# A fused SSD and attention layer: transposing normalised tokens, and V and dt as float32r products

## The chip, the cores and the metric

The kernel runs on one core of one Trainium2 chip. The metric is the device time of one execution in microseconds (us); shown are the median of three runs and their ends. The engines are called as in the profile: PE (matrix products, with PEld for its weight loads), DVE (vector), ACT (scalar), POOL (GpSimd) and SP (which only issues transfers here).

## The reference, cut

One layer over 512 tokens of width 1024, batch 1. A norm and one wide projection feed a two-way state-space scan (SSD) and a windowed attention; their outputs are gated, merged, projected and added to x; a squared-ReLU MLP follows. The change works on the first norm and on two of the projection's column groups, `dt_raw` and `v`.

```python
def rmsnorm(x, g):
    y = xf * lax.rsqrt(jnp.mean(xf * xf, axis=-1, keepdims=True) + EPS)
    return y * g

h = rmsnorm(x, pre_mix_norm[l])
proj = h @ w_in[l]
z, xbc, dt_raw, q, k, v, gates = split_cols(proj, IN_SPLITS)
y_ssd = ssd_branch(z, xbc, dt_raw, ..., w_ssd_out[l])
y_attn = window_attention(q, k, v, ...) @ w_attn_out[l]
mixed = (sigmoid(gates_ssd) * y_ssd + sigmoid(gates_attn) * y_attn) @ w_o[l]
x = x + rmsnorm(mixed, post_mix_norm[l])
f = square(relu(rmsnorm(x, pre_mlp_norm[l]) @ w_mlp_in[l])) @ w_mlp_out[l]
x = x + rmsnorm(f, post_mlp_norm[l])
```

## The kernel before

**Products.** Activations stand transposed, 128 features by 512 tokens per tile, eight tiles for a width of 1024. Nearly every large product is made from float32r operands: each operand is split into a high part (a cast to float32r on ACT, line 404 or 465) and a low part (the original less the high part, on DVE at line 405 or on POOL at line 469), and `mm3` (line 393) adds three products, high by high, high by low, low by high. V and dt are plain float32 products.

**Order.** The program is a list of quanta (groups of matmuls with the weights they need). `prefetch` loads weight chunks of 512 KB on SP's queue into a ring of three raw tiles and splits them into rings `wh` and `wl` of three. A Planner (line 64) then takes all instructions, costs them, lists them for each engine, and `chain` (line 490) fixes that order by dependencies. Working tiles of 128 x 512 come from 83 numbered slots.

**The start.** `start` (line 538) sends the identity and the norm's weight over ACT's queue, x and the four pieces `wv` of the V weights over SP's, and lets PE multiply zeros 20 times. For each of four token tiles, `turn_x` (line 583) transposes raw x in eight pieces, and ACT and DVE scale each by the norm's weight, which stands per partition in `gT`, into `xg` (lines 594, 596). `norm_x` (line 598) makes sums of squares on ACT and DVE and the reciprocal root `rst` on POOL (lines 608, 609). `v_quantum` (line 706) multiplies `xg` by `wv`, 32 products of 128 x 256, and scales by `rst` on the way out (line 722). `normal_h` (line 611) spreads `rst` over a tile `ra`, transposes it, multiplies it with `xg` and splits into `h`, in pieces of 128 x 256. `dt_quantum` (line 728) makes 32 products of 64 columns from `xg`, and `dt_math` (line 748) scales them by `rst`. Behind dt come the projection's other columns in chunks, K first.

**The seam to y.** When the last projection columns are done, the 16 slots of `h` are given back, and `split_y` (line 1246) splits the scan's output `yT` (16 tiles) into `yh` and `yl` (lines 1254, 1255) for the product with `w_ssd_out`. `flip_h2` (line 1366) fills 16 slots `h2`, the MLP's input, later.

## Time and profile before

| | us |
|---|---|
| median of three runs | 1096.55 |
| lowest, highest | 1095.93, 1097.31 |
| the profiled execution | 1097.11 |
| its span in the profile | 1095.3 |
| PE, POOL, DVE, ACT busy in it | 1083.8, 771.3, 759.7, 640.5 |
| first product of a projection chunk | 34.37 |
| start of the products with y | 623.36 |

Times in the rows are microseconds from the start of the span unless marked ns. A row of the timeline reads: start, time taken, engine, line, operation, output and inputs by the program's names, shapes, count, and in brackets the idle time of the engine ahead of it and what ended it. A row of the view by groups has count, then busy time and the mean of one in ns, then idle time ahead. A row of the waits has the engine that waits, for whom, total us, times, longest.

### The profile page before, as it was taken

To read this page: it belongs to the slowest core of one execution; us is meant where nothing else is said; L and a number is where in the kernel's file an instruction comes from. 1 tells how busy PE (TensorE), PEld (TensorE's weight loads), DVE (VectorE), ACT (ScalarE), POOL (GpSimd) and SP (SyncE) were. 2 spreads that over 40 slices of the span, in tenths; PEclk is the share of its full clock that TensorE was granted. 3 is DMA by queue.
4 is the path that set the end of the run, shared out by engine and by line. 5 is a ranking of instruction groups with operands and counts; after the bars stand their busy time and mean duration, and the time that the engine had idled before them with its cause. 6 is when DMAs were issued, how large, how long until landed. Compare 5 with 4: busy or idle time off the path is not lost. (4 is left out here: it accounts for less than half of the span.)

```text
span 1095.3 us, 16847 instructions
## 1 busy us (share of the span) xinstructions
PE 1083.8 (99%) x5647; PEld 910.1 (83%) x5647; DVE 759.7 (69%) x1319; ACT 640.5 (58%) x1387; POOL 771.3 (70%) x960
## 2 busy tenths in 40 slices
PE   9999999999999999999999999999999999999997
PEld 8887888888888888888888878888888888888886
DVE  5777887888796787886878843335653655755787
ACT  6467777687766777676678622323655444444543
POOL 2446657657568898999899866523668978978853
PEclk9999999999999999999999999999999999999999
DMA  6443624535535546556574563534311621621532
GB/s 206 123 121 104 146 79 140 132 82 146 137 99 168 156 141 167 152 146 165 141 189 124 175 201 97 163 100 161 117 43 53 193 69 48 193 74 43 165 102 77
DMA packets 214658, 140.66 MB, mean 128 GB/s; under 512 B 11779, under 2 KB 193523, under 8 KB 214572
## 3 DMA queue, kind: packets, MB, share of 16 engines
q1 hardware_dynamic: 214412, 139.53, 44.8%
q8 instruction: 44, 0.72, 0.3%
q14 instruction: 42, 0.34, 0.1%
q10 hardware_dynamic: 160, 0.07, 0.0%
HBM read 130.85 MB, written 8.72 MB: 127 GB/s over the span
## 5 line engine op out<-in xcount | busy, mean ns | idle before, releaser
L469 POOL TENSOR_TENSOR wl<-wr,wh 128x256 fp32r<-128x256 f32 (+1 forms) x500 | 412.1, 853 | 161.0 <-ACT wh L465 151.7
L387 PE MATMUL pp<-h,wh 128*128 128x512 f32 (+1 forms) x1712 | 524.2, 387 | 0.5 <-DVE h L1350 0.5
L387 PEld LDWEIGHTS pp<-h,wh 128*128 128x128 f32 x1712 | 316.4, 188 | 63.3 <-issue 1.0
L387 PE MATMUL pp<-h,wl 128*128 128x512 f32 (+1 forms) x856 | 331.9, 388 | 0.0
L465 ACT CAST wh<-wr 128x1024 fp32r<-128x1024 f32 x131 | 136.4, 1041 | 91.2 <-PE pp L387 79.0
L387 PEld LDWEIGHTS pp<-h,wl 128*128 128x128 f32 x856 | 160.8, 188 | 32.2 <-issue 0.3
L1517 POOL TENSOR_TENSOR wl<-wd,wh 128x256 fp32r<-128x256 f32 x140 | 114.2, 845 | 34.8 <-ACT wh L1513 31.6
L1513 ACT CAST wh<-wd 128x512 fp32r<-128x512 f32 x80 | 47.2, 620 | 51.3 <-PE pp L387 18.2
L387 PE MATMUL ps<-wh,fh 128*128 128x512 f32 (+1 forms) x196 | 75.5, 385 | 0.5 <-DVE acc L1563 0.5
L387 PE MATMUL ps<-wl,fh 128*128 128x512 f32 (+1 forms) x196 | 75.4, 385 | 0.0
L387 PE MATMUL ps<-wh,fl 128*128 128x512 f32 (+1 forms) x196 | 75.4, 385 | 0.0
L1393 DVE SCALAR_TENSOR_TENSOR pp<-pp,r 128x512 f32<-128x512 f32 (+1 forms) x31 | 17.6, 567 | 65.2 <-ACT r L1390 65.2
L1132 ACT ACTIVATE n<-cb,tables 128x128 f32<-128x128 f32 x128 | 49.1, 390 | 16.7 <-DVE cb L1123 14.6
L1517 POOL TENSOR_TENSOR wl<-wt,wh 128x256 fp32r<-128x256 f32 x56 | 45.5, 848 | 8.6 <-ACT wh L1513 4.9
L387 PE MATMUL pp<-yl,wh 128*128 128x512 f32 x128 | 50.0, 390 | 1.0 <-DVE yl L1255 1.0
L1168 POOL TENSOR_TENSOR w<-w,E 128x256 f32<-128x256 f32 x48 | 42.1, 891 | 12.3 <-DVE w L1164 5.9
L964 DVE SCALAR_TENSOR_TENSOR u<-pp,cv,u 128x510 f32<-128x510 f32 (+1 forms) x64 | 47.7, 745 | 3.3 <-ACT u L960 2.1
L387 PE MATMUL pp<-yh,wh 128*128 128x512 f32 x128 | 49.8, 389 | 0.0
L387 PE MATMUL pp<-yh,wl 128*128 128x512 f32 x128 | 49.8, 389 | 0.0
L1133 ACT ACTIVATE m<-cb,tables 128x128 f32<-128x128 f32 x128 | 48.8, 388 | 0.0
L1062 POOL TENSOR_TENSOR xd<-x,tables 128x256 f32<-128x256 f32 x48 | 35.5, 757 | 17.6 <-ACT x L987 14.7
L884 ACT ACTIVATE P<-P,mx 128x384 f32<-128x384 f32 (+1 forms) x64 | 35.2, 552 | 17.5 <-DVE mx L881 12.4
(240 smaller groups left out, 2147.9 us busy)
## 6 DMA issues: line engine op xcount, KB each, us to landing
wr<-in_w_in SPq DMA_DIRECT2D x74, 512.0 KB, 4.3
wr<-in_w_mlp_in SPq DMA_DIRECT2D x32, 512.0 KB, 4.6
wd<-in_w_mlp_out SPq DMA_DIRECT2D x64, 256.0 KB, 2.6
rb<-csT SPq DMA_DIRECT2D x32, 256.0 KB, 4.6
rf<-csT SPq DMA_DIRECT2D x32, 256.0 KB, 5.5
wr<-in_w_ssd_out SPq DMA_DIRECT2D x14, 512.0 KB, 4.5
E<-csE SPq DMA_DIRECT2D x96, 64.0 KB, 4.1
x<-in_x SPq DMA_DIRECT2D x16, 256.0 KB, 4.8
```

The lines of the kernel that those rows point to most:

```text
L387: self.nc.tensor.matmul(out, lhsT, rhs, start=start, stop=stop, skip_group_check=more)
L465: self.nc.scalar.copy(hi[:, :m], raw)
L469: engines[e].tensor_tensor(lo[:, c], raw[:, c], hi[:, c].bitcast(F32), op=ALU.subtract)
L884: nc.scalar.activation(p[:, :w], p[:, :w], AF.Exp, bias=mx[:, n:n + 1], accum_out=sm[:, n:n + 1])
L964: nc.vector.scalar_tensor_tensor(u[:, a:e], ps[:, a + d:e + d], self.wtap(t, b), u[:, a:e], op0=ALU.mult, op1=ALU.add)
L1062: nc.gpsimd.tensor_tensor(v4(xd[:, d * 256:(d + 1) * 256]), v4(xs(c)), by_dir(self.coef, c)[:, d].unsqueeze(2).to_broadcast([128, 4, 64]), ...
L1132: nc.scalar.activation(v4(n)[:, h], cb[:, 0], AF.Copy, scale=dt[:, 0, h:h + 1])
L1133: nc.scalar.activation(v4(m)[:, h], cb[:, 1], AF.Copy, scale=dt[:, 1, h:h + 1])
L1168: nc.gpsimd.tensor_tensor(wc, wc, E[:, d], op=ALU.add)
L1393: nc.vector.scalar_tensor_tensor(dst[:, tok], ps[:, tok], 0.0, r[:, tok], op0=ALU.max, op1=ALU.mult)
L1513: nc.scalar.copy(hi, w)
L1517: (nc.vector if e == "v" else nc.gpsimd).tensor_tensor(low[:, q], w[:, q], hi[:, q].bitcast(F32), op=ALU.subtract)
```

## The change

The norm's weight is loaded as two rows of 512 and spread over all partitions by two products with a column of ones, into two banks `gb`. DVE multiplies x by its root and by `gb` in one instruction for 512 columns (into `junk`), and these normalised tokens are transposed. The results go straight from the banks, by a cast on ACT and a subtraction on DVE, into four wide tiles `b`, 128 x 4 x 512 each, two for the high parts of h and two for the low parts. `turn_x`, `normal_h`, `xg` and `gT` go away.

V is made from h by three float32r products, with `wv` split by a cast on ACT and a subtraction on POOL; dt by two, over a chunk that holds the high and low weights side by side (mode "both") and comes through the ring. The four wide tiles are taken again for tiles 6 to 13 of y and again for `h2`. There are 13 products of zeros in place of 20 and 67 slots in place of 83.

```diff
@@ -24,10 +24,10 @@
-SLOTS, RAW, SPL, PP, AHEAD, SPARE = 83, 3, 3, 3, 4, 6
+SLOTS, RAW, SPL, PP, AHEAD, SPARE = 67, 3, 3, 3, 4, 6
 LO_DOWN = "p", "p", "p", "vp"
-WARM = 20
+WARM = 10
...
@@ -424,6 +424,15 @@
     def add(self, *quanta):
         self.quanta.extend(quanta)
+    def wide(self):
+        t = []
+        for i in range(4):
+            a = self.sp.tile([128, 4, 512], F32R, tag=f"b{i}", name=self.name("b"), bufs=1)
+            self.tags[a.tensor.name] = f"b{i}", 1
+            t.append(a)
+        return t, [(t[k // 4][:, k % 4], t[2 + k // 4][:, k % 4]) for k in range(8)]
     def twin(self, name):
         return self.slots.get(name + "h", dtype=F32R), self.slots.get(name + "l", dtype=F32R)
@@ -540,15 +549,16 @@
         get, put = self.slots.get, self.slots.put
         self.ident = self.const("ident", [128, 128])
         nc.scalar.dma_start(self.ident, self.d_cst[:, :128])
-        g = get("g", (128, 128))
-        nc.scalar.dma_start(g[:8], self.d_pre_mix_norm[0].rearrange("(k p) -> k p", p=128))
+        g = [get("g") for _ in range(2)]
+        for j in range(2):
+            nc.scalar.dma_start(g[j][:1], self.d_pre_mix_norm[0:1, j * 512:(j + 1) * 512])
         self.mhalf = self.const("mhalf", [128, 1])
         nc.vector.memset(self.mhalf, -0.5)
         self.ssq0 = self.const("ssq0", [128, 8])
         self.rst0 = self.const("rst0", [128, 4])
-        self.gT = self.const("gT", [128, 8])
-        self.zero = get("zero", (128, 128))
+        self.zero, one = get("zero", (128, 128)), get("one", (128, 128))
         nc.vector.memset(self.zero, 0.0)
+        nc.vector.memset(one[:1], 1.0)
         dummy = self.bank("ps")
         for _ in range(WARM):
             self.mm(dummy[:, :128], self.zero, self.zero, True, True)
@@ -560,40 +570,28 @@
                 nc.sync.dma_start(self.x0[t][j], self.d_x[0, t * 128:(t + 1) * 128, j * 512:(j + 1) * 512])
         def load_v(k):
-            w = get("wv", (128, 2, 256))
+            w, hi, lo = (get("wv", (128, 2, 256), d) for d in (F32, F32R, F32R))
             nc.sync.dma_start(w, self.d_w_in[k * 128:(k + 2) * 128, C_V:C_V + 256].rearrange("(k p) n -> p k n", p=128))
-            self.wv.append(w)
+            nc.scalar.copy(hi, w)
+            nc.gpsimd.tensor_tensor(lo, w, hi.bitcast(F32), op=ALU.subtract)
+            put(w)
+            self.wv.append((hi, lo))
         load_x(0)
         for k in range(0, 8, 2):
             load_v(k)
         for t in range(1, NT):
             load_x(t)
-        pg = self.bank("ps")
-        self.tr(pg[:, :8], g[:8, :])
-        nc.vector.tensor_copy(self.gT, pg[:, :8])
-        put(g)
-        self.xg = [get("xg") for _ in range(8)]
-        self.h = [(get("h", dtype=F32R), get("h", dtype=F32R)) for _ in range(8)]
-        self.turn_x(0)
+        self.gb = [self.bank("pp") for _ in range(2)]
+        for j in range(2):
+            self.mm(self.gb[j], one[:1], g[j][:1], True, True)
+        for _ in range(3):
+            self.mm(dummy[:, :128], self.zero, self.zero, True, True)
+        put(one, *g)
+        self.hb, self.h = self.wide()
         self.norm_x(0)
         self.prefetch(0)
         self.at(1, self.later_constants)
-
-    def turn_x(self, t):
-
...
     def norm_x(self, t):
@@ -604,27 +602,19 @@
         junk = [get("junk") for _ in range(2)]
         nc.scalar.activation(junk[0], x[0], AF.Square, scale=D ** -0.5, accum_out=ssq[:, 0:1])
         nc.vector.tensor_tensor_reduce(junk[1], x[1], x[1], 1.0 / D, EPS, ALU.mult, ALU.add, ssq[:, 1:2])
-        put(*junk, *x)
         nc.gpsimd.tensor_tensor(r, ssq[:, 0:1], ssq[:, 1:2], op=ALU.add)
         nc.gpsimd.tensor_tensor(r, r, self.mhalf, op=ALU.pow)
-
-    def normal_h(self, t2):
-
...
+        tok = slice(t * 128, (t + 1) * 128)
+        for j in range(2):
+            nc.vector.scalar_tensor_tensor(junk[j], x[j], r, self.gb[j], op0=ALU.mult, op1=ALU.mult)
+            ps = self.bank("ps")
+            for k in range(4):
+                self.tr(ps[:, k * 128:(k + 1) * 128], junk[j][:, k * 128:(k + 1) * 128])
+            hi, lo = (a[:, :, tok] for a in self.hb[j::2])
+            self.split(hi, lo, ps.rearrange("p (k t) -> p k t", k=4))
+        put(*junk, *x)
+        if t == 3:
+            put(self.zero)
     def later_constants(self):
         cst = self.const("cst", [128, 384])
@@ -709,41 +699,34 @@
         def run(_):
             if t < 3:
-                self.turn_x(t + 1)
                 self.norm_x(t + 1)
-            if t > 1:
-                self.normal_h(t - 2)
             tok = slice(t * 128, (t + 1) * 128)
-            ps = self.bank("pp")
-            for k in range(8):
-                self.mm(ps[:, :256], self.xg[k][:, tok], self.wv[k // 2][:, k % 2], k == 0, k == 7)
+            ps = self.bank("ps")
+            for a, b in ((0, 0), (1, 0), (0, 1)):
+                for k in range(8):
+                    self.mm(ps[:, :256], self.h[k][a][:, tok], self.wv[k // 2][b][:, k % 2], a + b + k == 0, b == 1 and k == 7)
             if t % 2 == 0:
                 self.V.append(self.slots.get("V", (128, 2, 256)))
-            nc.scalar.activation(self.V[t // 2][:, t % 2], ps[:, :256], AF.Copy, scale=self.rst0[:, t:t + 1])
+            nc.scalar.copy(self.V[t // 2][:, t % 2], ps[:, :256])
             if t == 3:
-                self.slots.put(*self.wv)
+                for a in self.wv:
+                    self.slots.put(*a)
         return Quantum([], run)
     def dt_quantum(self):
-        get, put = self.slots.get, self.slots.put
-
-        def load():
-            self.wdt = get("wdt", (128, 8, 64))
-            self.nc.sync.dma_start(self.wdt, self.d_w_in[:, C_DT:C_DT + 64].rearrange("(k p) n -> p k n", p=128))
-
-        def run(_):
+        def run(parts):
             ps = self.bank("ps")
             for t in range(NT):
+                tok = slice(t * 128, (t + 1) * 128)
                 for k in range(8):
-                    self.mm(ps[:, t * 64:(t + 1) * 64], self.xg[k][:, t * 128:(t + 1) * 128], self.wdt[:, k], k == 0, k == 7)
-            put(self.wdt)
-            put(self.zero, *self.xg)
-            self.dt_math(ps)
-
-        self.at(0.5, load)
-        return Quantum([], run)
+                    hi, lo = self.h[k]
+                    self.mm(ps[:, t * 128:(t + 1) * 128], hi[:, tok], parts[0][:, k], k == 0, False, True)
+                    self.mm(ps[:, t * 128:t * 128 + 64], lo[:, tok], parts[0][:, k, :64], False, k == 7, True)
+            self.dt_math(ps.rearrange("p (t n) -> p t n", t=4))
+        return Quantum([(self.d_w_in[:, C_DT:C_DT + 64].rearrange("(k p) n -> p k n", p=128), 8, 64, "both")], run)
     def dt_math(self, ps):
         nc = self.nc
@@ -756,9 +739,8 @@
         self.dt, self.cs, self.dec, self.coef = (self.tables[i // 2][:, i % 2] for i in range(4))
         w = [get("dtw", (128, 4, 64)) for _ in range(6)]
         v, e, r, s2, p, al = w
-        for t in range(NT):
-            nc.vector.scalar_tensor_tensor(v[:, t], ps[:, t * 64:(t + 1) * 64], self.rst0[:, t:t + 1], bias[:, 0],
-                                           op0=ALU.mult, op1=ALU.add)
+        nc.vector.tensor_tensor(v, ps[:, :, :64], bias[:, 0].unsqueeze(1).to_broadcast([128, 4, 64]), op=ALU.add)
+        nc.vector.tensor_tensor(v, ps[:, :, 64:], v, op=ALU.add)
         nc.scalar.activation(e, v, AF.Abs)
         nc.scalar.activation(e, e, AF.Exp, scale=-1.0)
@@ -1246,11 +1228,10 @@
     def split_y(self, k0, k1):
         nc = self.nc
         if k0 == 0:
-            for hi, lo in self.h:
-                self.slots.put(hi, lo)
+            self.wy = self.wide()[1]
             self.slots.put(*self.tables)
         for k in range(k0, k1):
-            hi, lo = self.slots.get("yh", dtype=F32R), self.slots.get("yl", dtype=F32R)
+            hi, lo = self.wy[k - 6] if 6 <= k < 14 else self.twin("y")
             nc.scalar.copy(hi, self.yT[k])
             nc.vector.tensor_tensor(lo, self.yT[k], hi.bitcast(F32), op=ALU.subtract)
             self.slots.put(self.yT[k])
@@ -1266,7 +1247,7 @@
         self.slots.put(t, self.gate[8 + m])
         self.mix.append((hi, lo))
         if m == 7:
-            for a in self.ys:
+            for a in self.ys[:6] + self.ys[14:]:
                 self.slots.put(*a)
             for k in range(0, 8, 2):
                 self.split_wo(1, k)
@@ -1367,7 +1348,7 @@
         nc = self.nc
         if t2 == 0:
-            self.h2 = [tuple(self.slots.get("h2", dtype=F32R) for _ in range(2)) for _ in range(8)]
+            self.h2 = self.wide()[1]
         tok = slice(t2 * 256, (t2 + 1) * 256)
         for k in range(0, 8, 2):
             ps = self.bank("ps")
@@ -1397,9 +1378,6 @@
             return
         self.combine(part, i // 2)
         self.slots.put(r)
-        if (part, i) == (3, 7):
-            for h in self.h2:
-                self.slots.put(*h)
     def combine(self, part, k):
```

On every engine the order moves in the start. On DVE, ACT and SP it moves around the seam to y too, and in the last 40 us, where the loads of the last norm's weight go out later. From the first products of the K columns on, PE and POOL have the same order in both, but that five of these products now stand ahead of dt.

PE, from its first instruction; before (`zero` the products of zeros, `ident,x` transposes, `pp_232` and `pp_284` V of the first two token tiles):

```order
L387 MATMUL ps_81<-zero_79 128x128 x20
L391 MATMUL ps_126<-ident,g_72 128x8
L391 MATMUL ps_153<-ident,x_102 128x128 x4
L391 MATMUL ps_154<-ident,x_103 128x128 x4
L391 MATMUL ps_208<-ident,x_114 128x128 x4
L391 MATMUL ps_209<-ident,x_115 128x128 x4
L387 MATMUL pp_232<-wv_106,xg_129 128x256
```

and in the changed kernel, the same place, with `pp_135` and `pp_136` the spread weight, `junk` the normalised tokens, `ps_217` and `ps_281` V of the first two token tiles; the first rows up to V, then the end of the first V:

```order
L387 MATMUL ps_84<-zero_80 128x128 x13
L387 MATMUL pp_135<-g_72,one_81 128x512
L387 MATMUL pp_136<-g_73,one_81 128x512
L391 MATMUL ps_153<-ident,junk_146 128x128 x4
L391 MATMUL ps_161<-ident,junk_147 128x128 x4
L391 MATMUL ps_202<-ident,junk_195 128x128 x4
L391 MATMUL ps_210<-ident,junk_196 128x128 x4
L387 MATMUL ps_217<-wv_100,b_142 128x256 x2
...
L387 MATMUL ps_249<-hot_245,tab_244 16x512
L387 MATMUL ps_217<-wv_119,b_143 128x256 x2
L391 MATMUL ps_266<-ident,junk_259 128x128 x4
```

The transposes now read a DVE result, and the last two products of the first V, which read the low part of the fourth piece, stand behind the bias table's product and ahead of the transposes of tile 2.

POOL, from its first work; before, the four pairs for `rst` stand in a row, and the first weight chunk follows:

```order
L608 TENSOR_TENSOR rst_77<-ssq_76 128x1
L609 TENSOR_TENSOR rst_77<-rst_77,mhalf 128x1
L469 TENSOR_TENSOR wl_180<-wr_177,wh_179 128x256 x4
```

and in the changed kernel, behind the pairs of tiles 0 and 1:

```order
L576 TENSOR_TENSOR wv_101<-wv_99,wv_100 128x512
L576 TENSOR_TENSOR wv_107<-wv_105,wv_106 128x512
L576 TENSOR_TENSOR wv_113<-wv_111,wv_112 128x512
L576 TENSOR_TENSOR wv_119<-wv_117,wv_118 128x512
L605 TENSOR_TENSOR rst_79<-ssq_78 128x1
L606 TENSOR_TENSOR rst_79<-rst_79,mhalf 128x1
L469 TENSOR_TENSOR wh_170<-wr_168,wh_170 128x8x64
```

The four low parts of the V weights stand ahead of the pair of tile 2, and the low part of the dt weights (`wh_170`) ahead of that of tile 3.

DVE, at the end of the products with h; before (`yl` low parts of y, `ol` of the weights w_o, `sl` of a sum of squares):

```order
L1255 TENSOR_TENSOR yl_7304<-yT_6934,yh_7303 128x512
L405 TENSOR_TENSOR ol_7595<-or_7515,oh_7594 128x512
L1255 TENSOR_TENSOR yl_7296<-yT_6331,yh_7295 128x512
L405 TENSOR_TENSOR ol_7447<-or_7379,oh_7446 128x512
L1255 TENSOR_TENSOR yl_7276<-yT_5100,yh_7275 128x512
L405 TENSOR_TENSOR sl_7162<-ssq_6975,sh_7161 128x512
```

and in the changed kernel (`b_7255` to `b_7258` are the wide tiles, now with y):

```order
L405 TENSOR_TENSOR sl_7166<-ssq_6979,sh_7165 128x512
L1236 TENSOR_TENSOR b_7257<-yT_5104,b_7255 128x512
L1236 TENSOR_TENSOR b_7257<-yT_5107,b_7255 128x512
L1236 TENSOR_TENSOR b_7257<-yT_5718,b_7255 128x512
L1236 TENSOR_TENSOR b_7257<-yT_5721,b_7255 128x512
L1236 TENSOR_TENSOR b_7258<-yT_6332,b_7256 128x512
L1236 TENSOR_TENSOR b_7258<-yT_6335,b_7256 128x512
L405 TENSOR_TENSOR ol_7504<-or_7448,oh_7503 128x512
L1236 TENSOR_TENSOR b_7258<-yT_6935,b_7256 128x512
```

The subtractions of tiles 6 to 13 of y, spread among others before, now stand together behind `sl`.

27 lines of the change are left out of this document (removed).

## The prediction

> **What bounds the kernel now.** I read the busy shares first, then the waits of TensorE, then the stretch of the span in which the change works.
>
> ```profile
> PE 1083.8 (99%) x5647; PEld 910.1 (83%) x5647; DVE 759.7 (69%) x1319; ACT 640.5 (58%) x1387; POOL 771.3 (70%) x960
> PE ps L387 <- ACT pT L901: 1.5, 2, 1.1
> PE ps L387 <- DVE zero L551: 1.0, 1, 1.0
> PE pp L387 <- DVE yl L1255: 1.0, 1, 1.0
> ...
> 8.03:34.37 26.34, 26.34 (x170) 23.34 (x170) 20.42 (x52) 17.35 (x50) 11.96 (x18) 1.00 0.71 203
> ```
>
> TensorE (PE) is busy for 99% of the span, and the waits that the view lists are 1.5 us or less. The last row is from the view by windows (length, busy time of PE, its weight loads, DVE, ACT and POOL with their instructions, granted clock, DMA share, GB/s): from the transpose of the norm's weight (8.03) to the first product of the first projection chunk (34.37), PE is busy for all of its 26.34 us, at a clock of 1.00. The other engines have slack there. So an edit is worth what it does to PE's time, and a new wait of PE costs its full length. From 34.37 on, the order of PE and POOL is the same in both kernels to the end. The change is therefore worth the shift of that one moment, plus what happens at the seam where y takes the place of h (about 620), plus the tail.
>
> **The start, part by part.** These are the rows of the timeline that price it, first those of the places, then those of the durations.
>
> ```profile
> 1.03 7.06 PE L387 MATMUL ps<-zero 128*128 128x128 f32 x40 [1.03 <-DVE zero L551]
> 1.15 0.57 ACTq L544 DMA_DIRECT2D g<-in_pre_mix_norm  x1
> 1.75 1.28 ACT L605 ACT_TABLE_LOAD   x1 [1.75 <-issue]
> 4.23 0.63 ACT L605 ACTIVATE junk<-x 128x512 f32<-128x512 f32 x1 [1.20 <-DMA x<-in_x]
> 4.89 0.69 DVE L606 CUSTOM_DVE_ANT_0 junk<-x 128x512 f32<-128x512 f32 x1 [3.68 <-DMA x<-in_x]
> 5.75 0.19 POOL L608 TENSOR_TENSOR rst<-ssq 128x1 f32<-128x1 f32 x1 [5.32 <-DVE ssq L606]
> 6.02 0.55 POOL L609 TENSOR_TENSOR rst<-rst,mhalf 128x1 f32<-128x1 f32 x1
> 8.18 1.97 PE L391 MATMUL ps<-ident,x 128*128 128x128 f32 x16
> 9.98 4.05 PE L387 MATMUL pp<-wv,xg 128*128 128x256 f32 x18
> 13.96 1.03 PE L387 MATMUL ps<-hot,tab 33*16 33x512 f32 x2
> 19.75 0.38 PE L391 MATMUL ps<-ident,ra 128*128 128x128 f32 x2
> 19.97 3.62 PE L387 MATMUL pp<-wv,xg 128*128 128x256 f32 x16
> 23.42 0.38 PE L391 MATMUL ps<-ident,ra 128*128 128x128 f32 x2
> 27.30 7.26 PE L387 MATMUL ps<-wdt,xg 128*128 128x64 f32 x64
> 34.37 0.71 PE L387 MATMUL pp<-h,wh 128*128 128x512 f32 x2
> ...
> 770.24 4.79 PE pp L387 x40
> ...
> L469 POOL TENSOR_TENSOR wl<-wr,wh 128x256 fp32r<-128x256 f32 x12 | 9.8, 847 | 3.5 <-ACT wh L465 3.5
> L465 ACT CAST wh<-wr 128x1024 fp32r<-128x1024 f32 x131 | 136.4, 1041 | 91.2 <-PE pp L387 79.0
> 627.11 2.78 POOL L469 TENSOR_TENSOR wl<-wr,wh 128x1024 fp32r<-128x1024 f32 x1 [2.43 <-ACT wh L465]
> 679.34 0.69 DVE L1262 SCALAR_TENSOR_TENSOR gate<-gate,pp 128x512 f32<-128x512 f32 x1 [6.47 <-PE pp L387]
> ```
>
> A float32 product leaves two records, a float32r product one. A stretch's time is taken from its start to the start of the next, since the ends of matmuls are modelled.
>
> *Removed from PE.* Eight V products (16 records) take 23.42 − 19.97 = 3.45 us, so one costs 0.431 and all 32 cost 13.8 us. The two pairs of `ra` transposes cost 0.22 each (19.75 to 19.97), 0.44 together, and the transpose of the weight 0.15 (8.03 to 8.18). dt takes 34.37 − 27.30 = 7.07 us, 64 passes of 0.1105.
>
> *Added on PE.* V is now 96 float32r products of 256 columns. The chain of waits shows forty products of that width in 4.79 us, 0.120 each: 11.5 us, and V saves 2.3. dt is now 64 float32r products, 32 with 128 moving columns and 32 with 64. No row has a narrow float32r product among such weight loads. The bounds are the passes of today's dt, which load 128 columns and move 64, at 0.1105 (7.07 us, a change of 0), and the 256-wide product at 0.120 (7.7 us, +0.6). I take +0.3, and come back to a cheaper price under the rivals. The 32 transposes stay, at (9.98 − 8.18)/16 = 0.1125 each, 0.45 for four.
>
> *The dummies and the spread of the weight.* Forty records of dummies last from 1.03 to 8.03. The changed kernel has 13 dummies, 26 records. At the mean of 0.175 they end at 5.6; since the early ones are the slower ones I take 6.3. Each spread is a float32 product of 512 columns with one row of weights; at twice the price of 256 columns it takes 0.86 (the bias table's, of that width, is 1.03 with its modelled end). They end at 7.2 and 8.0. That is when PE has its first real work today (8.03), so the dummies cost nothing and save nothing. ACT's queue now issues three transfers ahead of its table load, one more at 0.57: the load ends at 1.75 + 0.57 + 1.28 = 3.6, before x comes (4.23), and PE reads the weight's rows 5 us after their issue.
>
> *The new chain before the transposes.* Today they wait for x alone. Now they wait for squares, the root on POOL and a product on DVE. The root of tile 0 is done at 6.57 (6.02 + 0.55). The second spread is the later one for the first product, as are the squares of tile 1, which DVE makes first and which I let end at 7.3. The nearest row to the new product is DVE's scalar_tensor_tensor on a bank, 0.69. The four of tiles 0 and 1 then end near 8.1, 8.8, 9.5 and 10.2, and the last transposes at 10.8 with the hop between engines. So V of tile 0 starts at 10.8 where it started at 9.98: PE has idled 10.8 − 8.0 − 16 × 0.1125 = 1.0 us.
>
> *POOL, and what is queued behind its new work.* POOL now takes the low parts of the V weights, four pieces of 128 x 512, and they stand ahead of the root of tile 2. One piece costs 2.78/2 = 1.39 by the whole chunk and 2 × 0.847 = 1.69 by the rows of quarter chunks. From 8.25 on (behind the root of tile 1) the four end at 13.8 to 15.0. Two things wait for that. The last two products of V of tile 0 read the fourth piece: V and the bias table's product would be through at 10.8 + 24 × 0.12 + 0.86 = 14.5. The root of tile 2 follows on POOL with 0.19 + 0.55 = 0.74, then DVE's product of 0.69 and a hop of 0.2, so the transposes of tile 2 start at 15.4 to 16.6, and PE idles 0.9 to 2.1. Twice, in tiles 2 and 3, the second half waits 0.24 for its DVE product (0.69 against 0.45). Together with the first wait this is 2.4 to 3.6 us.
>
> DVE and POOL stretch each other here. The rows of the next fence show one DVE subtraction at 2.88 while POOL works on three pieces, against a mean of 1.17. DVE now has four subtractions of tiles 0 and 1 in this stretch; one such stretch delays both by up to 1.2. I put the new idle time of PE at 2.4 to 4.8 and take 3.6, nearer the slower piece, since that row is from this stretch.
>
> *What hides the rest.* ACT's four casts of weights and POOL's pieces were not there before; apart from the two waits named they lie under V. The split of h straight from the banks replaces scaling, spreading and splitting: DVE and ACT have 20.42 and 17.35 of 26.34 us busy there today and lose more than they gain. The dt weights now take a place in the ring of weight chunks, so the first chunk of Q waits for dt. dt ends near 36.5, with the first five products of the K columns now ahead of it; the cast of that chunk takes 1.04 and POOL's four quarters 3.4, so it is ready near 41. PE has 43 products of K left at 0.227 and comes to it near 46. Without that cover the 4.4 us would be PE's. The load of the dt weights moves on SP's queue from its own place to the ring's, one transfer for one.
>
> **The seam of y.** The wide tiles of h are free only after the last product that reads them. The first two can be written 12 products before that, the last two only at its very end, and then eight DVE subtractions for y stand in a row.
>
> ```profile
> 618.87 5.80 POOL L469 TENSOR_TENSOR wl<-wr,wh 128x256 fp32r<-128x256 f32 x3
> 620.09 2.88 DVE L405 TENSOR_TENSOR sl<-ssq,sh 128x512 fp32r<-128x512 f32 x1
> 622.75 0.39 PE L387 MATMUL ps<-sh,ones_r 128*128 128x512 f32 x1
> 623.36 0.40 PE L387 MATMUL pp<-yh,wh 128*128 128x512 f32 x1
> 624.41 0.57 ACT L1190 COPY rstd<-ps 1x512 f32<-1x512 f32 x1
> 639.69 3.45 DVE L1207 SCALAR_TENSOR_TENSOR yT<-w,cv,rstd 128x256 f32<-128x256 f32 x4 [8.64 <-DMA rstd<-rrow]
> 643.80 0.50 PE L387 MATMUL pp<-yl,wh 128*128 128x512 f32 x1 [0.98 <-DVE yl L1255]
> L1255 DVE TENSOR_TENSOR yl<-yT,yh 128x512 fp32r<-128x512 f32 x16 | 18.2, 1173 | 2.8 <-ACT yh L1254 2.7
> ```
>
> The h products end at 622.75, and y starts at 623.36, three products (0.68 us) for each k. Tiles 6 to 13 are the ones in question: k = 6 is wanted at 623.36 + 6 × 0.68 = 627.4, k = 13 at 632.2. DVE can begin them at about 621.3 (2.7 before 622.75, a cast like the copy's 0.57, and some 0.6 for what stands ahead), and eight at 1.17 are through at 630.7: the first with 5 us of slack, the last with 1.5. Two stretched subtractions (2.88 and 2.33 stand in this place today) use that up and leave a wait of up to 1.5. On the other side, ACT has fewer casts ahead of the copy at 624.41, which starts the trip of rstd through memory that ends in the wait of 0.98 at 643.80; it can shrink to nothing. From −1.0 to +1.5, I take 0.
>
> **The tail.** The loads of the last norm's weight go out later, behind a PE product 113 before the last. They would land some us before DVE wants them, and everything behind the last matmul is unchanged: 0.
>
> **The sum.** −2.3 (V) − 0.6 (`ra`, weight) + 0.3 (dt) + 3.6 (new idle time) + 0 + 0 = **+1.0 us**. With all the low bounds it is −2.9 + 0 + 2.4 − 1.0 = −1.5, with all the high ones −2.9 + 0.6 + 4.8 + 1.5 = +4.0. The profiled execution took 1097.11 us for a span of 1095.3, so 1.8 lie around the span and stay. It stands 0.56 above the median of 1096.55, so I add the difference to the median: **1097.6 us**.
>
> **The rivals.**
>
> *Narrow float32r products cost by their moving columns.* From 512 columns (0.227, 5.44 us for 24) and 256 columns (0.120) a line gives 0.067 for 128 and 0.040 for 64, so dt takes 32 × 0.107 = 3.4 us, the sum is −2.3 − 0.6 − 3.7 + 3.6 = −3.0, and the time 1093.6. Against it speak the weight loads:
>
> ```profile
> 826.42 5.44 PE ps L387 x24
> ...
> L387 PEld LDWEIGHTS pp<-h,wh 128*128 128x128 f32 x1712 | 316.4, 188 | 63.3 <-issue 1.0 <-DVE h L1350 0.7 <-ACT x L987 0.2
> L387 PEld LDWEIGHTS pp<-yh,wl 128*128 128x128 f32 x128 | 24.0, 188 | 5.0
> L387 PEld LDWEIGHTS ps<-wdt,xg 128*128 128x128 f32 x64 | 7.2, 192 | 0.0
> L387 PEld LDWEIGHTS ps<-pT,V 128*64 128x64 f32 x320 | 17.4, 137 | 1.4 <-issue 0.7 <-DVE rf L1129 0.4
> ```
>
> A load of 128 columns lasts 188 ns for float32r and 192 for float32, and 64 columns fewer save 51 ns, so 128 columns alone need about 0.10 us. A pass that moves only 64 columns, as dt's does, is set by that and not by its columns. 0.07.
>
> [...]
>
> *The seam stalls.* Casts into the wide tiles wait for PE on ACT, the weight casts queue behind them, and y's eight subtractions run at the stretched price. The price is the 1.5 above and as much as 0.5 from the next ones behind, so +2.0 on the forecast: 1099.6. It decides once the eight take over 11 us (630.7 + 1.5 is when k = 13 is wanted) and is slower than before. 0.18.
>
> *The clock falls in the new gaps.* Between 8 and 17 us PE would be busy for about 60% where it is busy throughout today. If the granted clock dropped for one stretch of the 13 us, V of tile 0 and the bias product (3.8 us) would take up to twice as long: +1.7 to +3.4, so 1100.1 with the middle. Today transposes alone (8.18 to 9.98) are followed by V at its full rate with the clock at 1.00, which speaks against it. 0.10.
>
> [...]
>
> *The change does not reach the end.* V's saving and the new waits cancel, or POOL's pieces go at 1.39 and the seam gains: the time is 1096.0, no change. 0.07.
>
> **How the numbers follow.** The forecast has 0.58. Two tenths of a per cent, 2.2 us, is about what a measurement of this kernel tells from no change: below 1094.4 is faster, above 1098.7 slower. Of the forecast's 0.58 I give 0.43 to no change, 0.13 to slower and 0.02 to faster. Faster is 0.02 + 0.07 (narrow products) = 0.09; slower is 0.13 + 0.18 + 0.10 = 0.41; the rest, 0.43 + 0.07 = 0.50, is no change. The range runs from 1094.6 (the low bounds less a little of the first rival) to 1101.0 (the high bounds, 1100.6, and both slow rivals but for their ends). The likeliest case alone spans 1096.0 to 1099.0.
>
> **What would show it.** V: 96 records at 0.12 apart. dt: 64 records in 7.1 to 7.7 us; 3.4 would be the first rival. The first products of the K columns, five of which now run ahead of dt: their start, with those five taken off what follows, lies 1.0 behind 34.37. Idle time of PE ahead of the transposes of tile 2, released by DVE's product, with POOL's four pieces ending at 13.8 to 15.0. At the seam a wait of PE on the y tiles, or none, and the wait of 0.98 at yl. The granted clock from 8 to 17. I am wrong in the main step if POOL's root of tile 2 comes before 14, if dt is far from 7, or if over 2 us appear after 40 us.

## The result: slower by 0.4%, and the profile after

The changed kernel takes 1101.91 us (median of 8 runs, 1098.8 to 1102.22), the kernel before 1096.93 in the same comparison (8 runs, 1095.53 to 1098.93). The ratio is 1.0037 (95% interval 1.0024 to 1.0050): slower by about 4 us. Five single executions in the comparisons below took far longer than the others of their kernel (1200 to 5956 us); the ratios leave them out, the medians do not. The profiled execution took 1102.03 us, for a span of 1100.0.

First the page of the changed kernel and the waits of its TensorE, as they were shown of before:

```profile
PE 1088.0 (99%) x5664; PEld 914.4 (83%) x5664; DVE 746.4 (68%) x1285; ACT 636.6 (58%) x1364; POOL 774.0 (70%) x965
```

```profile
PE ps L391 <- DVE junk L609: 1.2, 2, 1.1
PE ps L387 <- DVE zero L560: 1.0, 1, 1.0
PE pp L387 <- DVE yl L1236: 0.8, 1, 0.8
```

PE is as busy as before, 99%, and waits no more than before. Yet the span is 4.7 us longer, and PE's busy time 4.2. The time is not in more waiting: PE took longer over its work, though the change was to save it some. The timeline of PE through the start shows where.

```profile
8.71 3.35 PE L391 MATMUL ps<-ident,junk 128*128 128x128 f32 x16 [0.16 <-DVE junk L609]
11.72 3.45 PE L387 MATMUL ps<-wv,b 128*128 128x256 f32 x22
15.10 1.03 PE L387 MATMUL ps<-hot,tab 33*16 33x512 f32 x2
17.65 1.29 PE L391 MATMUL ps<-ident,junk 128*128 128x128 f32 x8 [1.08 <-DVE junk L609]
18.69 3.12 PE L387 MATMUL ps<-wv,b 128*128 128x256 f32 x24
22.61 5.99 PE L387 MATMUL ps<-wv,b 128*128 128x256 f32 x48
28.44 0.63 PE L387 MATMUL pp<-b,wh 128*128 128x512 f32 x2
29.72 10.43 PE L387 MATMUL ps<-wh,b 128*128 128x128 f32 x64
39.96 0.77 PE L387 MATMUL pp<-b,wl 128*128 128x512 f32 x1
```

The 64 records of dt reach from 29.72 to 39.96, 10.24 us, where before 64 passes took 7.07. The view by windows has the reason in its granted clock (columns as in the prediction, here of PE alone: stretch, length, busy time with records, clock, DMA share, GB/s):

```profile
8.71:11.72 3.01, 2.98 (x16) 0.65 1.06 335
28.44:33.00 4.56, 4.56 (x39) 1.00 0.75 209
33.50:39.96 6.46, 6.46 (x32) 0.50 0.01 3
39.96:43.50 3.54, 3.54 (x10) 0.50 0.00 0
43.50:62.49 18.99, 18.99 (x85) 0.99 0.31 83
```

The clock is at half speed from 33.5 to 43.7, in the midst of a PE that is never idle there. The edges come from the same view in windows of half a microsecond:

```profile
9.50:10.00 0.50, 0.50 (x4) 0.59 1.06 370
13.00:13.50 0.50, 0.50 (x6) 0.99 0.99 168
33.00:33.50 0.50, 0.50 (x7) 0.99 0.00 0
43.50:44.00 0.50, 0.50 (x3) 0.77 0.00 0
```

The windows of half a microsecond within each fall read 0.50, those around it 1.00. If the clock stood at one or the other throughout (an estimate from these readings), a mean of 0.59 is 0.41 us at half and the rest whole. So there are two falls, from 9.59 to 13.01 and from 33.49 to 43.73. The second lasts 10.24 us, three times 3.41, and the first 3.41 as well, to the hundredth that such edges can be off.

Where the 4.7 us are, from the starts of the same instructions in the two traces:

| | before | after | shift |
|---|---|---|---|
| dt begins (after: less the five K products, 1.13, that now stand ahead) | 27.30 | 28.59 | +1.3 |
| dt itself | 7.07 | 10.24 | +3.2 |
| products of K and behind, up to K with Q (after: from 39.96, with the five added: 22.53 + 1.13) | 21.87 | 23.66 | +1.8 |
| first product of K with Q | 56.24 | 62.49 | +6.25 in all |
| first long run of products of pT with V | 94.86 | 99.05 | +4.2: 2.0 come back |
| sum of squares ahead of y | 622.75 | 626.88 | +4.1 |
| first y product that waits for yl | 643.80 | 647.62 | +3.8 |
| end of the span | 1095.3 | 1100.0 | +4.7 |

So the loss is dt (+3.2) and the products behind it, which run at half clock up to 43.73 (+1.8). The start gives +1.3, a wait near 88 that is gone takes 2.0 back, and the seam of y takes 0.3.

### The profile page after: what moved, and what is told of

Same layout as the page of the kernel before. It is cut to its first block, busy times and chain, and to the rows that moved or that the text cites. A ratio compares the mean times of both kernels' runs of the same rounds, so it can differ in the third digit from the quotient of the medians.

```text
span 1100.0 us, 16840 instructions
## 1 busy us (share of the span) xinstructions
PE 1088.0 (99%) x5664; PEld 914.4 (83%) x5664; DVE 746.4 (68%) x1285; ACT 636.6 (58%) x1364; POOL 774.0 (70%) x965
## 4 chain that ended last, share of the span: by engine, by line
PE 96%; DMA 2%; DVE 1%; issue 0%; POOL 0%; POOLq 0%; DVEq 0%; SPq 0%
PE pp L387 67%; PE ps L387 26%; PE ps L391 4%; DMA wd<-in_w_mlp_out 1%; DMA rstd<-rrow 0%; DVE yT L1189 0%; DVE x L1575 0%; DVE acc L1541 0%; DVE junk L609 0%; DVE ag L1568 0%; DVE wd L1459 0%; DVE yl L1236 0%; POOL wl L478 0%; POOLq L1662 0%; DVE wd L1460 0%
## 5 line engine op out<-in xcount | busy, mean ns | idle before, releaser
L387 PE MATMUL pp<-b,wh 128*128 128x512 f32 (+1 forms) x1840 | 565.1, 388 | 0.8 <-DVE h L1331 0.8
L387 PEld LDWEIGHTS pp<-b,wh 128*128 128x128 f32 x1840 | 341.3, 188 | 68.8 <-issue 1.0
L387 PE MATMUL pp<-b,wl 128*128 128x512 f32 (+1 forms) x920 | 357.7, 389 | 0.0
L387 PEld LDWEIGHTS pp<-b,wl 128*128 128x128 f32 x920 | 173.4, 189 | 34.9 <-issue 0.3
L1114 ACT ACTIVATE n<-cb,tables 128x128 f32<-128x128 f32 x128 | 49.5, 394 | 16.6 <-DVE cb L1105 14.1
L866 ACT ACTIVATE P<-P,mx 128x384 f32<-128x384 f32 (+1 forms) x64 | 35.3, 555 | 17.3 <-DVE mx L863 12.2
L1110 ACT ACTIVATE rf<-rf,tables 128x128 f32<-128x128 f32 x128 | 42.5, 396 | 2.4 <-DMA rf<-csT 2.3
L387 PEld LDWEIGHTS ps<-wh,fh 128*128 128x128 f32 x196 | 36.8, 188 | 8.0 <-DVE acc L1541 0.7
L387 PEld LDWEIGHTS ps<-wh,fl 128*128 128x128 f32 x196 | 36.8, 188 | 7.4
```

The source lines that it names most:

```text
L387: self.nc.tensor.matmul(out, lhsT, rhs, start=start, stop=stop, skip_group_check=more)
L1110: nc.scalar.activation(v4(rf)[:, h], v4(rf)[:, h], AF.Identity, bias=ncs[:, 0, h:h + 1])
L1114: nc.scalar.activation(v4(n)[:, h], cb[:, 0], AF.Copy, scale=dt[:, 0, h:h + 1])
```

## The experiments

The theory after the first reading: dt's 64 narrow float32r products (narrow: few moving columns) keep the array in use for so small a part of some 3.41 us, the length that the two falls have in common, that the clock goes to 0.50 (a guess from those lengths, to be tested), and the products of K behind them still pay. The rivals: narrow float32r products simply cost 0.16 us each; or the clock falls because of what is changed earlier, the gaps of PE in the start. All ratios are to the kernel before, with 95% intervals.

**dt with 512 moving columns.** The weights stand still and h moves:

```diff
-            for t in range(NT):
-                tok = slice(t * 128, (t + 1) * 128)
-                for k in range(8):
-                    hi, lo = self.h[k]
-                    self.mm(ps[:, t * 128:(t + 1) * 128], hi[:, tok], parts[0][:, k], k == 0, False, True)
-                    self.mm(ps[:, t * 128:t * 128 + 64], lo[:, tok], parts[0][:, k, :64], False, k == 7, True)
-            self.dt_math(ps.rearrange("p (t n) -> p t n", t=4))
+            for k in range(8):
+                hi, lo = self.h[k]
+                self.mm(ps, parts[0][:, k], hi, k == 0, False, True)
+                self.mm(ps, parts[0][:, k], lo, False, k == 7, True)
+            turned, pt = self.slots.get("dtT"), self.bank("ps")
+            self.nc.scalar.copy(turned, ps)
+            for t in range(NT):
+                self.tr(pt[:, t * 128:(t + 1) * 128], turned[:, t * 128:(t + 1) * 128])
+            self.slots.put(turned)
+            self.dt_math(pt.rearrange("p (t n) -> p t n", t=4))
```

> The changed kernel with dt turned round: the weights stand still (128 columns, high and low side by side), h moves in 16 products of 512 columns, and four transposes bring the result back. Theory (the clock falls because 64 narrow float32r products keep PE too little occupied for a whole 3.4 us window): dt takes 16 x 0.227 = 3.6 us in place of 10.24, the granted clock stays at 1.00 from 30 to 45, the K products run at 0.227 at once; the first product of K with Q (62.49 in the changed kernel, 56.24 before) comes near 54 to 55, and the time falls by 5 to 7 us, to 0.998 to 0.999 of before. Rival (narrow products simply cost 0.16 each, and the clock falls for a reason that lies earlier, the gaps in the start): dt shrinks by the same 6.6 us, but the clock still falls to 0.50 for about 10 us near 33 and takes 3 to 5 us back; the time falls by 2 to 4.

Measured: 1094.31 us, ratio 0.9972 (0.9961 to 0.9983), 3 us faster than before and some 7 faster than the changed kernel. The timeline and the windows of PE:

```profile
29.09 3.90 PE L387 MATMUL ps<-b,wh 128*128 128x512 f32 x16
32.83 0.39 PE L387 MATMUL pp<-b,wl 128*128 128x512 f32 x1
```

```profile
13.00:29.00 16.00, 14.89 (x113) 1.00 0.73 200
29.09:32.83 3.74, 3.74 (x20) 1.00 0.63 163
32.83:53.00 20.17, 20.17 (x92) 1.00 0.30 80
```

dt takes 3.74 us, the clock stays whole behind it, and K with Q begins at 53.95. The second rival, which wanted the fall all the same, is out: the first fall (8.5 to 11.9 here) is still there, and no second one follows.

**dt in float32.** The same place, shape and number of passes as before, from the high parts alone:

```diff
-                    self.mm(ps[:, t * 128:(t + 1) * 128], hi[:, tok], parts[0][:, k], k == 0, False, True)
-                    self.mm(ps[:, t * 128:t * 128 + 64], lo[:, tok], parts[0][:, k, :64], False, k == 7, True)
+                    self.mm(ps[:, t * 128:t * 128 + 64], self.h[k][0][:, tok].bitcast(F32), parts[0][:, k, :64].bitcast(F32), k == 0, k == 7)
...
-        nc.vector.tensor_tensor(v, ps[:, :, 64:], v, op=ALU.add)
```

> The changed kernel with dt as 32 plain float32 products of 64 columns from the high parts alone (64 passes; the low parts of h and of the dt weights are left out), everything else the same. Theory (narrow float32r products are what the clock's watch counts as idle; a float32 pass of 64 columns occupies PE for longer): dt takes 64 x 0.1105 = 7.1 us at a granted clock of 1.00, and K with Q comes near 57.5. Rival (any stretch of products bound by weight loads, or the gaps before it, lets the clock fall): dt takes about 10 us, and the clock is 0.50 for about 10 us as in the changed kernel.

Measured: 1097.02 us, ratio 0.9998 (0.9989 to 1.0007). This is the whole change but for the form of dt's products (32 in float32, which are 64 passes, in place of 64 in float32r), and it is as fast as before: all of the loss hangs on that form.

```profile
28.99:36.06 7.07, 7.07 (x66) 1.00 0.26 78
36.06:56.00 19.94, 19.94 (x90) 1.00 0.30 79
```

dt takes 7.07 us at a whole clock, and K with Q begins at 56.82, 0.6 behind before. So the start without the fall in dt is nearly a draw.

**dt mixed with K.** The 64 narrow products as they are, with a product of K behind every three. In the planned order the first 15 still stand together.

```diff
...
+                for i, (u, v) in enumerate(((h, a[k][0]), (h, a[k][1]), (l, a[k][0]))):
+                    self.mm(ps, u, v, k == 0 and i == 0, k == nk - 1 and i == 2, True)
+                    for _ in range(3):
+                        if self.drip:
+                            self.mm(*self.drip.popleft())
...
```

> The changed kernel with the same 64 narrow products, but after the first 15 of them one 512-wide product of K stands between every three. Theory (occupation over a window decides): no window is filled with narrow products alone, the clock stays at 1.00 or falls for one window at most (3.4 us), the time falls by 3 to 5 us. Rival (the narrow products cost 0.16 each wherever they stand): no change within 1 us.

Measured: 1098.61 us, ratio 1.0011 (1.0002 to 1.0020). The clock fell once, from 8.7 to 12.1, and read 1.00 through the mixed stretch (in each window from 28 to 48); the time is some 3 us under that of the changed kernel. The rival that a narrow product costs 0.16 wherever it stands is out. That its profiled execution ends behind that of the float32 form is not the clock: K with Q begins at 57.16, 0.3 later, and the sums ahead of y 2.1 later. In between lies DVE, which begins dt's arithmetic at 40.48 in place of 36.29; that this is the cause is not shown. In three of the twelve runs the mean clock was 0.995 against 0.997 in the profiled one, so some of them may have had a longer fall.

**The same 64 products in the kernel before.** They are made once more behind the columns of K, and their result is not used.

```diff
+    def probe_quantum(self):
+        def run(parts):
+            ps = self.bank("ps")
+            for t in range(NT):
+                tok = slice(t * 128, (t + 1) * 128)
+                for k in range(8):
+                    hi, lo = self.h[k]
+                    self.mm(ps[:, t * 128:(t + 1) * 128], hi[:, tok], parts[0][:, k], k == 0, False, True)
+                    self.mm(ps[:, t * 128:t * 128 + 64], lo[:, tok], parts[0][:, k, :64], False, k == 7, True)
...
-        self.add(*[self.v_quantum(t) for t in range(NT)], self.dt_quantum(), *kv)
+        self.add(*[self.v_quantum(t) for t in range(NT)], self.dt_quantum(), *kv, self.probe_quantum())
```

> The kernel before, with the changed kernel's 64 narrow float32r products (32 of 128 and 32 of 64 moving columns, over h and the dt weights) made once more behind the K columns; their result is not used. Theory (such a row of narrow float32r products lets the clock fall by itself, whatever stood in the start): the clock is 1.00 through the start and falls to 0.50 within 7 us of their first; the added time is 7.1 us at full clock plus 3 to 6 us, so 1.009 to 1.012 of before. Rival (the changed start is needed for the fall): the clock stays at 1.00 and the added time is 7 us, 1.0065.

Measured: 1107.58 us, ratio 1.0093 (1.0074 to 1.0112). The timeline and windows of PE in this kernel:

```profile
44.42 10.15 PE L387 MATMUL ps<-wh,h 128*128 128x128 f32 x64
54.38 1.20 PE L387 MATMUL pp<-h,wh 128*128 128x512 f32 x2
```

```profile
5.00:44.00 39.00, 39.00 (x236) 1.00 0.63 175
44.42:48.00 3.58, 3.58 (x34) 1.00 0.58 146
48.50:58.00 9.50, 9.50 (x38) 0.50 0.20 55
59.00:68.00 9.00, 9.00 (x43) 1.00 0.22 58
```

The clock is whole for 39 us of gapless work. The narrow products come at 44.42 and it falls to 0.50 some 3.9 us later, for 10.25 us (48.31 to 58.56). They cost 9.96 us (54.38 − 44.42), near the 10.24 of the changed kernel, and the products behind them some more. The changed start is not needed for it.

**All of dt's products with 128 columns.** One slice less: the low part of h is multiplied with high and low weights alike, which adds the product of the two low parts.

```diff
-                    self.mm(ps[:, t * 128:t * 128 + 64], lo[:, tok], parts[0][:, k, :64], False, k == 7, True)
+                    self.mm(ps[:, t * 128:(t + 1) * 128], lo[:, tok], parts[0][:, k], False, k == 7, True)
```

> The changed kernel with all 64 dt products moving 128 columns (the low part of h is multiplied with high and low weights, which adds a term the changed kernel leaves out). At full clock a product costs 0.11 either way, so the array is in use for a larger part of the same 7.1 us: at 0.417 ns a column some 53 of 110 ns in place of 40 on the mean. Theory A (the watch wants more than half of a window in use): the clock falls as in the changed kernel, dt takes about 10 us, time as in the changed kernel, 1.002 to 1.005 of before. Theory B (it wants something between 0.36 and 0.48): no fall, dt 7.1 us, the time as with float32 dt, 0.999 to 1.001 of before.

Measured: 1096.98 us, ratio 0.9999 (0.9989 to 1.0009). Theory B: no second fall in the profile, and none of the ten runs has a mean clock under 0.996, where the profiled run of the changed kernel has 0.992.

```profile
28.00:36.00 8.00, 8.00 (x69) 1.00 0.34 96
36.00:45.00 9.00, 9.00 (x44) 1.00 0.22 59
```

dt reaches from 29.38 to 36.56, 7.18 us, 0.112 a product. More moving columns at the same price per product kept the clock whole. As an estimate, a column costs 0.417 ns in float32r (the line through 512 and 256 columns in the prediction) and 0.84 in float32 (0.2155 for a pass of 256). The part of the time in which the columns move is then 40 of 110 ns, 0.36, in the changed kernel; 53 of 112, 0.48, here; 54 of 110, 0.49, in the float32 form. The clock fell at the first and at neither of the others. If that share decides, the bound lies between 0.36 and 0.48, by the same estimate; these runs fit that but do not prove it. That a float32r product of 64 columns simply counts for less would fit them too.

**The changed kernel once more.**

> The changed kernel once more, for a second profile. If the falls follow a running window of 3.4 us, the falls begin and end at other places of the span than in the first profile (9.6 to 13.0 and 33.5 to 43.7), but at distances from each other that are multiples of about 3.4 us, and the dt stretch loses one to three windows. If they follow the instructions alone, they begin at the same instruction again.

Measured: 1102.78 us, ratio 1.0045 (1.0030 to 1.0061). In windows of half a microsecond the falls reach from 10.37 to 13.78 and from 34.26 to 44.5, all 0.8 later than in the first profile. The distances are the same, 3.41, 20.5 (six times 3.41) and 10.24. The windows of the second fall:

```profile
30.22:34.20 3.98, 3.98 (x39) 1.00 0.38 121
34.30:44.40 10.10, 10.10 (x40) 0.50 0.00 0
```

So the falls lie at other places of the span and at the same distances, as the first of the two cases has it. That they follow the instructions is not excluded by these two profiles, since dt moved by 0.5 as well.

The runs without a trace show that the fall is not of one length. Of the eight runs in the first comparison, six have a mean clock of 0.992 or 0.993 and take 1101.53 us or more; the two shortest, 1099.12 and 1098.80, have 0.996 and 0.995. As an estimate, 3.41 us at 0.50 take 0.0016 off the mean of a span of 1100 us and cost at most 1.7 us. By it these two stood at half for about twice 3.41 us less, which is worth their 3 us.

**The first fall: the norm's weight over 128 rows.** The product that spreads it reads one row; here 127 rows of zeros are added.

```diff
...
+            nc.gpsimd.memset(g[j], 0.0)
             nc.scalar.dma_start(g[j][:1], self.d_pre_mix_norm[0:1, j * 512:(j + 1) * 512])
...
-        nc.vector.memset(one[:1], 1.0)
+        nc.vector.memset(one, 1.0)
...
-            self.mm(self.gb[j], one[:1], g[j][:1], True, True)
+            self.mm(self.gb[j], one, g[j], True, True)
```

> The changed kernel with the norm's weight spread by products over 128 rows (127 of them zero) in place of one row; the same number of products and columns, all 13 products of zeros ahead of them. Theory (a product over one row counts as idle, which with the gaps before the transposes lets the clock fall from 9.6 to 13.0): the clock stays at 1.00 there, V of tile 0 ends about 0.7 us earlier, the fall in dt stays, the time falls by 0 to 0.7 us. Rival (the gaps between the transposes do it): the clock falls from about 9.6 as before, and the time stays within 0.5 us.

Measured: 1101.44 us, ratio 1.0036 (1.0024 to 1.0049), the ratio of the changed kernel. The fall between 8 and 13 is gone here, and in all four kernels that have this edit, while each of the six profiles with the one-row product shows it. The second fall stays. The price of the first fall can be read from the profiles. From the first transposes to the bias table's product PE takes 6.16 to 6.55 us in the six with the fall (8.71 to 15.10 in the changed kernel) and 5.47 to 5.73 in the four without, so the fall costs 0.4 to 1.1. The runs are too few to show so small a gain (1.0036 against 1.0037). Nor is the edit a sure cure: in the next kernel the clock fell once, later.

**Both cures.** The wide dt and the 128 rows together.

> The changed kernel with both cures: dt with 512 moving columns and the norm's weight spread by products over 128 rows. Theory (two separate falls of the clock, each cured by its own edit): the clock is 1.00 from 5 to 45, K with Q comes near 53, 1 us earlier than with the wide dt alone (53.95), and the time is 0 to 1 us under that kernel's, 0.996 to 0.997 of before. Rival (the early fall was covered by the wait for the root of tile 2, so curing it gives nothing): K with Q at 53.9, same time as with the wide dt alone.

Measured: 1093.28 us, ratio 0.9964 (0.9953 to 0.9975), within the interval of the wide dt alone (0.9961 to 0.9983). Its profile has a fall from 17.3 to 20.7, behind the wait for tile 2, and K with Q at 55.13, so it bears out neither theory: here the clock fell behind the second gap in the start, where six other profiles, with the product over one row, have it fall near the first. But the profiled run, at 1095.40 us and a mean clock of 0.996, is the slowest of the six that count. Four of the others have 0.998 or 0.999, as the profiles of the next two kernels have (0.998), in which each window from 5 to 70 us reads 1.00. So most runs of this kernel probably had no fall, as the first theory has it; without their traces that is not shown.

**The wait near 88.** Before, PE waited for ACT's copies of pT (rows of before, then of the kernel with the probe):

```profile
88.27 0.44 PE L387 MATMUL ps<-KH,Q 128*128 128x384 f32 x1 [1.13 <-ACT pT L901]
89.28 0.44 PE L387 MATMUL ps<-KH,Q 128*128 128x384 f32 x1 [0.39 <-ACT pT L901]
57.95 0.48 DVE L875 CUSTOM_DVE_ANT_0 P<-ps,bt,sink 128x256 f32<-128x256 f32 x1
```

```profile
68.70 0.48 DVE L888 CUSTOM_DVE_ANT_0 P<-ps,bt,sink 128x256 f32<-128x256 f32 x1 [1.23 <-PE ps L387]
```

Before, DVE came to the first row maxima 1.7 us after K with Q had begun (57.95 against 56.24), busy until then with the arithmetic of dt, and waited for nothing. With the probe PE comes 12 us later and DVE waits for PE (1.23). From the third group of K with Q to the run of pT with V it then takes 6.27 us (97.82 to 104.09) in place of 8.19 (86.67 to 94.86), and 6.15 in the changed kernel (92.90 to 99.05): the wait is gone, in a kernel that has none of the change. A later PE is not needed for that either: with the wide dt K with Q begins 2.3 us earlier than before (53.95), DVE comes 1.1 behind it (55.06), and the stretch takes 6.14 (84.34 to 90.48). To test the cause from the other side, DVE gets four more instructions in the kernel with both cures:

```diff
+        for _ in range(4):
+            nc.vector.tensor_scalar(self.dt, self.dt, 1.0, None, op0=ALU.mult)
         nc.scalar.activation(bias[:, 1], bias[:, 1], AF.Exp)
```

> The kernel with both cures and four more DVE instructions in the middle of the dt arithmetic (a multiplication by one, 128 x 256 each, some 1.2 to 1.7 us together), nothing on PE. Theory (before, PE's wait of 2.0 us at 88 came from DVE, which reached the first row maxima 1.7 us behind the first K with Q because its work in the start ended late; the changed start ends it sooner): DVE comes to the maxima over 2 us behind, the wait of PE for pT near 86 returns with 1 to 2.5 us, the time rises by as much against the kernel with both cures. Rival (that wait had another source, such as ACT's order or the table's transfer): no wait, the time within 0.5 us.

Measured: 1095.61 us, ratio 0.9986 (0.9977 to 0.9996), 2.4 us behind the kernel with both cures, with these waits of PE in its timeline:

```profile
53.32 0.38 PE L387 MATMUL ps<-KH,Q 128*128 128x256 f32 x1 [0.50 <-DVE Q L838]
55.64 0.73 PE L387 MATMUL pp<-b,wh 128*128 128x512 f32 x2 [0.87 <-ACT KH L812]
86.18 0.45 PE L387 MATMUL ps<-KH,Q 128*128 128x384 f32 x1 [0.40 <-ACT pT L887]
```

The size was right, the place hardly: 0.4 us at pT, where the kernel with both cures has 0.2, and 1.4 at Q and at KH, which stand behind the new work on DVE as well. The late DVE cost PE its time there. But DVE now came to the row maxima 2.9 us behind K with Q (56.18 against 53.32), later than before, and the stretch took 6.83 us (84.95 to 91.78), not 8.19. So the lag of DVE alone does not make the wait near 88, and its cause stays open.

**Two pieces of the V weights on DVE.** On top of both cures:

```diff
-            nc.gpsimd.tensor_tensor(lo, w, hi.bitcast(F32), op=ALU.subtract)
+            (nc.gpsimd if k < 4 else nc.vector).tensor_tensor(lo, w, hi.bitcast(F32), op=ALU.subtract)
```

> The kernel with both cures and the low parts of the last two pieces of the V weights on DVE in place of POOL, so that POOL comes to the root of tile 2 some 2.5 us earlier. Theory (the transposes of tile 2 wait for POOL's four pieces): the root of tile 2 ends near 13 in place of 15, the transposes of tile 2 start 0.5 to 1 us earlier, the time falls by 0.5 to 1 us against the kernel with both cures. Rival (DVE is then what they wait for, it now stands in two more subtractions): no change within 0.5 us, or up to 1 us slower.

Measured: 1091.55 us, ratio 0.9950 (0.9937 to 0.9963), the fastest of all: 5.5 us under before. Its interval overlaps that of both cures (0.9953 to 0.9975), so the 1.5 us between the two are not clear of noise. The transposes of tile 2 begin at 15.95 and no longer wait; with both cures alone they begin at 16.96 with a wait of 1.08. First the rows here, then those of both cures:

```profile
14.49 0.54 POOL L605 TENSOR_TENSOR rst<-rst,mhalf 128x1 f32<-128x1 f32 x1
15.06 1.40 DVE L608 SCALAR_TENSOR_TENSOR junk<-x,rst,pp 128x512 f32<-128x512 f32 x2
15.53 0.50 PE L387 MATMUL ps<-wv,b 128*128 128x256 f32 x2
15.95 1.29 PE L391 MATMUL ps<-ident,junk 128*128 128x128 f32 x8
17.59 0.68 DVE L687 COPY rows<-ps 16x512 f32<-16x512 f32 x1
```

```profile
15.28 0.54 POOL L605 TENSOR_TENSOR rst<-rst,mhalf 128x1 f32<-128x1 f32 x1
15.48 0.68 DVE L687 COPY rows<-ps 16x512 f32<-16x512 f32 x1 [0.37 <-PE ps L387]
16.09 1.38 DVE L608 SCALAR_TENSOR_TENSOR junk<-x,rst,pp 128x512 f32<-128x512 f32 x2
16.96 1.74 PE L391 MATMUL ps<-ident,junk 128*128 128x128 f32 x8 [1.08 <-DVE junk L608]
```

The root is ready at 15.03 in place of 15.82: 0.8 us earlier, and not at 13. POOL is through with its two pieces at 11.99 and then waits 1.90 us for DVE's squares, which end at 13.75 (13.92 with both cures). The theory is right in part. The other part is DVE's order: the copy of the bias table's rows, which stood ahead of DVE's product for tile 2, now stands behind it (17.59), so the product begins as soon as the root is there. Without the copy the product of both cures could have begun at 15.82 in place of 16.09 (an estimate), so most of the 1.0 us came from the earlier root. In the changed kernel, where the table's product ends later, the copy weighs more:

```profile
15.04 0.54 POOL L606 TENSOR_TENSOR rst<-rst,mhalf 128x1 f32<-128x1 f32 x1
16.17 0.68 DVE L688 COPY rows<-ps 16x512 f32<-16x512 f32 x1 [1.31 <-PE ps L387]
16.77 1.38 DVE L609 SCALAR_TENSOR_TENSOR junk<-x,rst,pp 128x512 f32<-128x512 f32 x2
```

The root was there at 15.58; DVE waited 1.31 us for PE's table product to copy it, and PE then waited for DVE.

## Why the prediction was right or wrong

On the scale of the prediction's 1096.55 the ratio gives 1100.6, within the range and near its upper end, and slower had 0.41. But the likeliest case, no change at +1.0, is not what happened, and most of the time went where the sum had +0.3. That the time lies in the range is luck: the half clock in dt and behind it cost 5.0 us, and 2.0 near 88, for which the sum had no term, came back. By its steps:

- **PE bounds, so the change is worth what it does to PE's time.** Right, and the views by busy share and by waits could not show the loss, since a PE at half clock counts as busy (6.46 of 6.46 us at 0.50, from 33.50 to 39.96).
- **V.** Right: the last 48 products take 28.44 − 22.61 = 5.83 us, 0.121 each.
- **The spread and the first transposes.** Right to 0.6 us for the first transposes (8.71 against some 8.1). V began at 11.72 in place of 10.8, 3.01 us behind them: the clock was at 0.65 on the mean in between, and with the spread over 128 rows, at a whole clock, it takes 2.39 (8.05 to 10.44).
- **POOL's four pieces ahead of the root of tile 2.** They ended at 14.8, within the forecast 13.8 to 15.0. The step from there failed: not the root but DVE's copy of the table's rows ended last, and the transposes began at 17.65 in place of 15.4 to 16.6. The prediction looked on POOL for what was queued ahead of this work, and not on DVE. Part of the delay is the first fall of the clock, ahead of the table's product: with the spread over 128 rows the transposes began at 16.08, inside the forecast.
- **The start without dt.** +1.3 where the terms gave +0.7 (3.6 − 2.3 − 0.6); in the kernel with float32 dt, K with Q began 0.6 behind before. Near, though the first fall, which the sum does not have, is part of it.
- **dt, +0.3.** This is the step that failed. "The bounds are the passes of today's dt ... and the 256-wide product" held for the price at a whole clock: the same number of products at 128 columns takes 0.112 each. What was wrong is that a price taken at a whole clock was carried to a stretch without asking whether the clock would stay so. It cost 3.2 us in dt and 1.8 in the products behind it.
- **The rival of narrow products by their columns (0.07).** Wrong, as the prediction itself argued: with twice the columns in every other product the price did not move (0.112 against 0.110).
- **The rival of the clock (0.10).** The mechanism was the right one and its place was wrong. It was looked for in the gaps between 8 and 17, and there the clock did fall, to 0.50 at 9.59, though PE had been idle for only 0.19 us from 8.00 to 9.50, at a price of 0.4 to 1.1 us by the profiles. The fall that counted came in a stretch without a gap. That its time, 1100.1, came close is luck: it is another sum.
- **The seam of y, 0, and the rival that it stalls (0.18).** No stall: PE waits for none of the wide tiles, and the wait at yl shrank from 0.98 to 0.81. Over the seam PE gained 0.3.
- **What hides the rest.** The Q chunk's cover held. But a wait of 2.0 us near 88 went away, for which the sum had nothing. The waits shown in the prediction have most of it, ACT pT with 1.5; it was read as too small to matter, and what stood behind ACT was not followed. A DVE that comes earlier is the likely part of the change, but that is argued: the test with a later DVE did not bring the wait back at its place.
- **The tail, 0.** The shift grows from +3.8 at yl to +4.7 at the end. The first 0.4 are two waits of PE for DVE's h: 0.79 at 765.28, where before has 0.54, and 0.24 at 771.38, where before has none. The last matmul begins 4.2 later (1092.42 against 1088.18), and another 0.5 comes behind it, from a cause that is open.

## What to carry to other kernels

A PE that is busy without a gap can still lose its full clock: 64 float32r products in a row with few moving columns, 7.0 us of them at a whole clock (64 at 0.110 each), brought it to 0.50 for 10.24 us in the profiles, and the wide products behind them paid too (1.8 us in the changed kernel). How short a stretch does it was not measured; 15 in a row, the others mixed with wide ones, did not. Ask of such a stretch for what part of each product's time its columns move (by the estimate above, 0.36 in the stretch that fell, 0.48 and 0.49 in the two that did not); make the moving side the wide one, or fill it (here 128 columns in place of 64 on every other product were worth some 4 us and cost nothing). Read the granted clock beside the busy time before looking for a wait, and when a wait is named, read the queue of the engine that it names too.

## What the runs showed of the hardware that was not expected

- Narrow float32r products (128 and 64 moving columns, 128 to load, 0.110 each at a whole clock) brought the clock to 0.50 in a gapless stretch, 3.8 to 4.3 us after the first of them in four of four profiles. Float32 passes of 64 columns at the same 0.110, and float32r products of 128 columns at 0.112, did not.
- In these four profiles the half clock lasted 10.24 or 10.25 us, three times 3.41. In each, the last 3.41 held 512-wide products alone (40.32 to 43.73 in the changed kernel, where these begin at 39.96), and the clock came back at its end.
- A product over one row, with gaps behind it, was followed by a fall in six of six profiles; over 128 rows in none of four at that place.
